# First feed-forward block of an encoder layer: one plain inner chunk instead of three, and one more unit of seven products

## The chip, the cores and the metric

The kernel runs on one core of one Trainium2 chip. A core has TensorE (PE in the profile, with PEld for its weight loads), VectorE (DVE), ScalarE (ACT), GpSimd (POOL) and SyncE (SP), each with its own in-order list of instructions, and 16 DMA engines that all of them share. The metric is the device time of one execution in microseconds (us).

## The reference

One layer of a bidirectional encoder on 512 tokens of width 1024, in float32. A conditioning vector gives nine shift, scale and gate vectors (`mod`); then come a gated feed-forward block, two attention mixers side by side, and a second feed-forward block. Only the first block is touched:

```python
mod = silu(c) @ w_mod + b_mod                # 9 vectors of 1024
h = rmsnorm(x, norm_ffn1) * (1 + sc1) + sh1
gate, up = split(h @ w_ffn1_in)              # 1024 x 5632: 2816 gate, 2816 up
x = x + 0.5 * g1 * ((silu(gate) * up) @ w_ffn1_out)
```

## The kernel before

**Products in three parts.** Activations lie with their features on the 128 partitions and the 512 tokens along the free axis. Every float32 operand of a large product is split into a rounded high part and a low part (`split_from`: ACT copies the high part, DVE subtracts it to get the low one), and a product is three matmuls: high by high, high by low, low by high (L174 to L176, 512 columns wide). A weight tile of 128x1024 comes by a DMA of 512 KB into a tile `raw` or `u`, and its parts go to one of four slots of two tiles `high` and `low` (L185 and L186 of the profile).

**The inner width.** The 2816 inner columns of the first block are 22 chunks of 128. For each chunk there are a gate product and an up product, both over the eight blocks of 128 features. Chunks 0 to 2 are computed in the opening, where DVE still works out the shift and scale vectors (L272, with the columns of `w_mod` as they arrive) and h itself (L346 to L351). After the opening come `PLAIN` pairs less the three chunks already done, computed plainly: in the kernel before, `PLAIN` is 3, so chunks 3, 4 and 5, each of 48 matmuls of 512 columns. `finish` then takes silu of the gate (ACT, L725), multiplies (DVE, L726) and splits the result.

**Units of seven products.** The rest goes in units, each of two chunks of gate and two of up. A unit splits weights and h into 2 by 2 blocks and forms its result by seven products of half the columns instead of eight, with sums of weight blocks and sums of h blocks as operands. Each product is 24 matmuls of 256 columns (L444 to L446). Its products and their h operands are `s1` by n1, `a11` by b11, `a12` by b21, `s2` by n2, `s3` by t3, `s4` by b22, `a22` by t4. The sums n1, n2, t3, t4 are formed once by DVE in `h_sum` (L574 and L576) and split. The sums of weights are made by DMAs that add: SP loads a21 into a tile (L478), POOL issues a DMA that adds a22 (L480), which gives s1; after s1 has been split, POOL issues another that adds a11 into the same tile, which gives s2, and after that one that adds a12, which gives s4; a21 added onto the tile of a11 gives s3 (all L499). After a product ACT copies its PSUM bank aside where it is needed later (L521), or DVE adds it to others (L523, L528, L531). The products a11, s2, s3 and a22 of one unit share one bank, so the matmuls of s2 wait for the copy of a11, and those of s3 for the copy of s2.

**Order.** SP and POOL issue in the order of the program. Instructions of PE, ACT and DVE in this part are ordered by the framework's scheduler when the kernel is built; on the chip each engine keeps that order. `run_items` goes through a written list of products; each has its load asked for (`ASK`) and its parts made (`MAKE`) some products ahead, and before each product `side1` adds 0.27 to a credit; a full credit loads one more column of `w_mod` into one of two places and works an earlier one off on DVE (L272). A third column load waits on SP until DVE has worked off the first.

**After the units.** The output product of the block (`Out1`, L174 to L176) runs over groups of chunks: 0 to 5, 6 to 11, 12 to 15, 16 to 21. In the kernel before, the list is unit 3, group one, units 4 and 5, group two, and so on to unit 10. One product of the next unit's `s1`, `a11` and `a12` stands among those of the current one.

Of the kernel before, what the change touches and what calls it, by code (L numbers as in the profile page):

```python
# [106 lines left out]
MIX_ASIDES = 0, 0, 0, 0, 0, 0, ASIDE, ASIDE  # L107

CHUNKS = (range(0, 6), range(6, 12), range(12, 16), range(16, 22))
PLAIN, LAST_1 = 3, 4  # L110


EARLY, NEXT, SIDE, LATER = 3, 3, 0.27, 4
# [21 lines left out]
def layer(ctx: ExitStack, tc: tile.TileContext, a: dict):  # L135
# [16 lines left out]
    def f2():  # L152
        return sbuf("f2", [P, T], F32, F2)

    def b8(dt=F32R):
        return sbuf("b8", [P, 4, T], dt, 12)

    def u4(dt=F32R):
        return sbuf("u4", [P, 2, T], dt, 6)
# [13 lines left out]
    def mm3(out, wh, wl, xh, xl, first, last):  # L173
        PE.matmul(out, wh, xh, start=first, stop=False)  # L174
        PE.matmul(out, wh, xl, start=False, stop=False)  # L175
        PE.matmul(out, wl, xh, start=False, stop=last)  # L176
# [7 lines left out]
    def split_from(hi, lo, src):  # L184
        S.copy(hi, src)  # L185
        V.tensor_tensor(lo, src, f(hi), ALU.subtract)  # L186
# [18 lines left out]
    def load_split(src, n=1024, spare=False, aside=0):  # L205
        raw = sbuf("raw", [P, 1024], F32, RAW)
        if spare:
            hi, lo = (u4().rearrange("p a b -> p (a b)") for _ in range(2))
        else:
            hi, lo = high_low(aside=aside)  # L210
        nc.sync.dma_start(raw[:, 0:n], src)
        split_from(hi[:, 0:n], lo[:, 0:n], raw[:, 0:n])
        return hi, lo
# [207 lines left out]
    def pair_banks():  # L421
        return (bank("acc"), bank("sc"))
# [111 lines left out]
    def run_items(items):  # L534

        due, at, now = [], [], 0.0  # L540
        for u, q, ks, also in items:
            at.append(now)
            for do, ahead in ((u.ask, u.ASK), (u.prepare, u.MAKE)):
                if q in ahead:
                    due.append((now - ahead[q], len(due), do, q))
            now += u.length
        due.sort(key=lambda d: d[0:2])

        def begin(n):

            for d in [d for d in due if d[0] <= at[n]]:
                _, _, do, p = d
                if do.__name__ == "ask" or p in do.__self__.ready or len(holders) < HILO:
                    due.remove(d)
                    do(p)

        for n, (u, q, ks, also) in enumerate(items):
            begin(n)
            if also is not None:
                also()  # L560
            u.multiply(q, ks)
            if ks is None or u.depth - 1 in ks:
                u.after(q)
            begin(n)
# [6 lines left out]
    def sub(out, p, q, negated):  # L571

        if negated:
            V.scalar_tensor_tensor(out, p, -1.0, q, ALU.mult, ALU.subtract)  # L574
        else:
            V.tensor_tensor(out, p, q, ALU.subtract)  # L576
# [10 lines left out]
    def h_sum(t):  # L587

        p, q = SUMS[t]
        hq[t] = hq[q if t in ("t3", "t4") else p]  # L590

        h_op[t] = [u4() for _ in range(2)] if t == "n1" else b8()
        for i in range(2):
            r = slice(i * T, (i + 1) * T)
            sub(hq[t][:, r], hq[p][:, r], hq[q][:, r], t in NEGATED)
        for i in range(2):
            v = hq[t][:, i * T : (i + 1) * T].rearrange("p (k q) -> p k q", k=2)
            o = h_op[t][i] if t == "n1" else h_op[t][:, 2 * i : 2 * i + 2, :]
            split_from(o[:, :, T1], o[:, :, T2], v)
# [118 lines left out]
    def act_of(p):  # L718
        if p not in act1:
            act1[p] = b8()  # L720
        return act1[p]

    def finish(q, out):
        s, m = f2(), f2()
        S.activation(s, out[0], AF.Silu)  # L725
        V.tensor_tensor(m, s, out[1], ALU.mult)  # L726
        t = act_of(q // 2)
        split_from(t[:, q % 2, :], t[:, 2 + q % 2, :], m)
# [23 lines left out]
    def in_unit1(p):  # L752
        srcs = {q: a["w1u"][p - PLAIN, i] for i, q in enumerate(("a11", "a12", "a21", "a22"))}
        u = Unit(srcs, 4, h1_operand, in_post1, p % 2)
        u.p, u.in_order = p, ('s2', 's4')
        return u
# [49 lines left out]

    items1 = []

    def item1(u, q, ks=None):
        items1.append((u, q, ks, side1))  # L810

    credit, asked = [0.0], []

# [3 lines left out]
    def column(columns):  # L817

        if columns:
            v, c = columns.pop(0)  # L820
            w = room[len(columns) % len(room)] if columns is not later else None
            asked.append((v, c, mod_load(v, c, w)))
        if asked and (len(asked) > COLUMNS[columns is rest] or not columns):
            mod_col(*asked.pop(0), in_order=columns is not later)

    def side1(n=SIDE):

        while small_loads and len(rest) < 20:
            nc.sync.dma_start(*small_loads.pop())
        credit[0] += n  # L830
        while (rest or asked) and credit[0] >= 1.0:
            credit[0] -= 1.0
            column(rest)

    with tc.manual_schedule(engines={mybir.EngineType.SP, mybir.EngineType.Pool}):
        for q in range(3):
            finish(q, out1[2 * q : 2 * q + 2])
        sums1 = ["n1", "n2", "t3", "t4"]
        units1 = {p: in_unit1(p) for p in range(PLAIN, NH)}
        for q in range(3, 2 * PLAIN):  # L840

            w = loaded1 or [load_split(a["w1i"][q - 3, k], aside=ASIDE * (q == 5)) for k in range(2)]
            loaded1 = None
            out = pair_banks()
            for k in range(NC):
                wh, wl = w[k // 4]
                for i in range(2):
                    o = (k % 4) * 256 + i * P
                    mm3(out[i], wh[:, o : o + P], wl[:, o : o + P], hh[k], hl[k], k == 0, k == NC - 1)
            for _ in range(2):  # L850
                if sums1:
                    h_sum(sums1.pop(0))
            finish(q, out)
            if q == 3:
                units1[PLAIN].ask("s1")
            elif q == 4:
                units1[PLAIN].prepare("s1")
            side1(1.0)
        begun = PLAIN
        for n, chunks in enumerate(CHUNKS):  # L860


            final = n + 1 == len(CHUNKS)
            for p in range(begun, max(chunks.stop // 2, PLAIN + 1)):
                u, nxt = units1[p], units1.get(p + 1)
                if p == PLAIN:
                    item1(u, "s1")
                    item1(u, "a11")
                elif p > begun:
                    item1(units1[p - 1], "a22")  # L870
                if p == PLAIN or p > begun:
                    item1(u, "a12")
                item1(u, "s2")
                if nxt:
                    item1(nxt, "s1")
                item1(u, "s3")
                item1(u, "s4")
                if nxt:
                    item1(nxt, "a11")
            item1(u, "a22")  # L880
            if nxt:
                item1(nxt, "a12")
            begun, nxt = p + 1, nxt or u
            out = Out1(chunks, "acc" if nxt.odd != final else "sc", final)
            if final:
                first = range(len(chunks) - 2)
                for m in range(2):
                    item1(out, m, first)
                for m in range(2):
                    item1(out, m, range(len(chunks) - 2, len(chunks)))  # L890
            for m in range(2 if final else 0, NC - LAST_1 if final else NC):
                item1(out, m)
        run_items(items1)
        last1 = []
        for m in range(NC - LAST_1, NC):
            out.prepare(m)
            last1.append((m, lambda po, r, m=m: out.products(m, po, r, range(out.depth))))
        while rest or asked:
            column(rest)
# [931 lines left out]
    u = units[2]  # L1831
# [19 lines left out]
    for v, p in seq:  # L1851
# [7 lines left out]
        u = v  # L1859
# [77 lines left out]
```

## Time and profile before

| | us |
|---|---|
| median of three runs | 1066.88 |
| lowest and highest | 1066.68, 1067.96 |
| span of the profiled execution | 1066.6 |
| PE busy in it | 1047.0 |
| DVE, ACT, POOL busy | 795.7, 566.6, 155.0 |

The page gives no other time for the profiled execution than its span, from the first to the last instruction, 0.28 us below the median. The granted TensorE clock is 1.00 throughout. Times in the text are microseconds from the start of the span.

In the timeline a row gives start, duration, engine, line, operation, output<-input and shapes, and in brackets the idle time of the engine before it with what ended it. Matmuls overlap: one of 512 columns is shown with 0.39 us, but starts follow each other by 0.227 to 0.234 us, and the starts are what counts.

### The profile page before, as it was taken

How to read it: one execution, taken by the hardware profiler on the slowest of the kernel's cores; microseconds unless marked ns; L12 is line 12 of the kernel's file. 1: busy time of each engine (PE TensorE's matmuls, PEld its weight loads, DVE VectorE, ACT ScalarE, POOL GpSimd, SP SyncE). 2: the span in 40 equal slices, each digit the busy share in tenths (PEclk: the TensorE clock that was granted, in tenths of full speed). 3: DMA queues.
4: the chain of work that ended last, by engine and by line, in shares of the span. 5: the costliest groups of instructions: out<-in, count | busy, mean ns of one | idle time of the engine just before them, and what ended most of it. 6: DMA issues, size and time to landing. Idle time of an engine off the chain costs nothing.

```text
span 1066.6 us, 18660 instructions
## 1 busy us (share of the span) xinstructions
PE 1047.0 (98%) x7316; PEld 953.3 (89%) x7316; DVE 795.7 (75%) x1459; ACT 566.6 (53%) x928; POOL 155.0 (15%) x174
## 2 busy tenths in 40 slices
PE   7999999999999999999999999999999999999998
PEld 5689889899899998888777878989999999999997
DVE  6985666666796679858864578976889777877867
ACT  5564334344354342667676755534766646654553
POOL 1100010100110100443211100001011211112210
PEclk9999999999999999999999999999999999999999
DMA  9968687866975459696356852974498998999974
GB/s 332 362 205 208 207 211 189 264 155 195 281 181 160 164 200 409 215 270 160 99 120 166 239 160 85 351 242 118 101 232 200 215 230 217 220 219 213 219 146 124
DMA packets 69084, 220.92 MB, mean 207 GB/s; under 512 B 8194, under 2 KB 10882, under 8 KB 68995
## 3 DMA queue, kind: packets, MB, share of 16 engines
q1 hardware_dynamic: 46512, 146.52, 38.2%
q0 software_dynamic: 19488, 68.70, 34.9%
q10 hardware_dynamic: 2994, 4.51, 1.2%
q8 instruction: 57, 0.93, 0.3%
q14 instruction: 33, 0.26, 0.1%
HBM read 209.46 MB, written 10.23 MB: 206 GB/s over the span
## 4 chain that ended last, share of the span: by engine, by line
PE 79%; DVE 8%; issue 5%; DMA 3%; ACT 3%; POOL 1%; SPq 0%; ACTq 0%; DVEq 0%; POOLq 0%
PE acc L444 5%; PE acc L446 5%; PE acc L445 5%; PE sc L174 5%; PE sc L175 5%; PE sc L176 5%; PE sc L446 5%; PE sc L444 5%; PE sc L445 5%; PE acc L174 4%; PE acc L176 4%; PE acc L175 4%; PE sc L182 2%; PE acc L1048 2%; PE acc L1049 2%
## 5 line engine op out<-in xcount | busy, mean ns | idle before, releaser
L185 ACT CAST high<-raw 128x1024 fp32r<-128x1024 f32 (+2 forms) x162 | 158.3, 986 | 165.9 <-PE acc L445 38.8
L186 DVE TENSOR_TENSOR low<-raw,high 128x1024 fp32r<-128x1024 f32 (+2 forms) x162 | 183.7, 1141 | 61.2 <-ACT high L185 60.2
L444 PE MATMUL acc<-b,high 128*128 128x256 f32 x508 | 141.0, 278 | 0.3 <-DVE f L523 0.3
L446 PE MATMUL acc<-b,low 128*128 128x256 f32 x508 | 140.6, 277 | 0.2 <-DVE low L186 0.2
L445 PE MATMUL acc<-b,high 128*128 128x256 f32 x508 | 140.6, 277 | 0.1
L444 PE MATMUL sc<-b,high 128*128 128x256 f32 x500 | 138.5, 277 | 1.8 <-ACT f L521 1.8
L446 PE MATMUL sc<-b,low 128*128 128x256 f32 x500 | 138.6, 277 | 1.1 <-DVE low L186 1.1
L445 PE MATMUL sc<-b,high 128*128 128x256 f32 x500 | 138.4, 277 | 0.0
L186 DVE TENSOR_TENSOR low<-u,high 128x1024 fp32r<-128x1024 f32 (+1 forms) x73 | 87.5, 1200 | 28.4 <-ACT high L185 27.1
L185 ACT CAST high<-u 128x1024 fp32r<-128x1024 f32 (+1 forms) x73 | 75.5, 1035 | 56.5 <-PE sc L175 15.9
L174 PE MATMUL sc<-b,high 128*128 128x512 f32 (+1 forms) x280 | 100.8, 360 | 0.0
L175 PE MATMUL sc<-b,high 128*128 128x512 f32 (+1 forms) x280 | 100.4, 359 | 0.0
L176 PE MATMUL sc<-b,low 128*128 128x512 f32 (+1 forms) x280 | 100.2, 358 | 0.0
L444 PEld LDWEIGHTS acc<-b,high 128*128 128x128 f32 x508 | 95.4, 188 | 0.8 <-DVE f L523 0.5
L444 PEld LDWEIGHTS sc<-b,high 128*128 128x128 f32 x500 | 94.0, 188 | 2.2 <-ACT f L521 2.2
L445 PEld LDWEIGHTS acc<-b,high 128*128 128x128 f32 x508 | 95.5, 188 | 0.4 <-DVE b L1725 0.3
L446 PEld LDWEIGHTS acc<-b,low 128*128 128x128 f32 x508 | 95.4, 188 | 0.4 <-DVE low L186 0.4
L446 PEld LDWEIGHTS sc<-b,low 128*128 128x128 f32 x500 | 93.9, 188 | 1.5 <-DVE low L186 1.5
L445 PEld LDWEIGHTS sc<-b,high 128*128 128x128 f32 x500 | 93.9, 188 | 0.0
L174 PE MATMUL acc<-b,high 128*128 128x512 f32 (+1 forms) x248 | 92.7, 374 | 0.0
L176 PE MATMUL acc<-b,low 128*128 128x512 f32 (+1 forms) x248 | 90.0, 363 | 0.0
L175 PE MATMUL acc<-b,high 128*128 128x512 f32 (+1 forms) x248 | 89.8, 362 | 0.0
(369 smaller groups left out, 2676.4 us busy)
## 6 DMA issues: line engine op xcount, KB each, us to landing
u<-w_mod SPq DMA_DIRECT2D x40, 512.0 KB, 7.6
b<-w_mod SPq DMA_DIRECT2D x32, 512.0 KB, 6.0
raw<-w2i SPq DMA_DIRECT2D x31, 512.0 KB, 5.9
u<-w2i POOLq DMA_DIRECT2D x31, 512.0 KB, 6.6
u<-w1u POOLq DMA_DIRECT2D x24, 512.0 KB, 7.1
raw<-w1u SPq DMA_DIRECT2D x24, 512.0 KB, 6.8
raw<-w1o SPq DMA_DIRECT2D x24, 384.0 KB, 4.5
raw<-w_gate SPq DMA_DIRECT2D x16, 512.0 KB, 6.8
```

The lines of the kernel that those rows point to most:

```text
L174: PE.matmul(out, wh, xh, start=first, stop=False)
L175: PE.matmul(out, wh, xl, start=False, stop=False)
L176: PE.matmul(out, wl, xh, start=False, stop=last)
L182: PE.matmul(out, of[j][a], of[j][b], start=i == 0, stop=i == 2)
L185: S.copy(hi, src)
L186: V.tensor_tensor(lo, src, f(hi), ALU.subtract)
L444: PE.matmul(out, wh[:, s], xh, start=first and j == 0, stop=False, skip_group_check=True)
L445: PE.matmul(out, wh[:, s], xl, start=False, stop=False, skip_group_check=True)
L446: PE.matmul(out, wl[:, s], xh, start=False, stop=last and j == 1, skip_group_check=True)
L1048: PE.matmul(out[t][:, 0:n], hh[k][:, ht], wh[:, o : o + n], start=k == 0, stop=False)
L1049: PE.matmul(out[t][:, 0:n], hh[k][:, ht], wl[:, o : o + n], start=False, stop=False)
```

## The change

`PLAIN` goes from 3 to 2. Chunk 3 alone is computed plainly; chunks 4 and 5 become unit 2. The units are now 2 to 10, nine instead of eight, and the list is unit 2, group one, units 3, 4 and 5, group two, and then as before. The loads of `w1i` for chunks 4 and 5 go (four of 512 KB); the loads and adding DMAs of a unit come (eight transfers of 512 KB).

With one chunk left, what stood between the three has to go elsewhere. The weights of the first unit's s1 are asked for before chunk 3 and made after it; n1 and n2 are formed at chunk 3, t3 before the product s1, t4 before a11. Of the three column loads, one now stands before chunk 3 and two after it.

```diff
-PLAIN, LAST_1 = 3, 4
+PLAIN, LAST_1 = 2, 4
...
-    def item1(u, q, ks=None):
-        items1.append((u, q, ks, side1))
+    def item1(u, q, ks=None, sums=None):
+        def do():
+            side1()
+            if sums:
+                h_sum(sums)
+
+        items1.append((u, q, ks, do))
...
             finish(q, out1[2 * q : 2 * q + 2])
+        side1(1.0)
         sums1 = ["n1", "n2", "t3", "t4"]
         units1 = {p: in_unit1(p) for p in range(PLAIN, NH)}
+        units1[PLAIN].ask("s1")
         for q in range(3, 2 * PLAIN):
...
             finish(q, out)
-            if q == 3:
-                units1[PLAIN].ask("s1")
-            elif q == 4:
-                units1[PLAIN].prepare("s1")
-            side1(1.0)
+            units1[PLAIN].prepare("s1")
+            side1(2.0)
...
                 if p == PLAIN:
-                    item1(u, "s1")
-                    item1(u, "a11")
+                    item1(u, "s1", sums="t3")
+                    item1(u, "a11", sums="t4")
```

## The prediction

> **What bounds the kernel now.** I read the totals of the page first, then the chain that ended last, then the waits of PE.
>
> ```profile
> span 1066.6 us, 18660 instructions
> PE 1047.0 (98%) x7316; PEld 953.3 (89%) x7316; DVE 795.7 (75%) x1459; ACT 566.6 (53%) x928; POOL 155.0 (15%) x174
> ...
> PE 79%; DVE 8%; issue 5%; DMA 3%; ACT 3%; POOL 1%; SPq 0%; ACTq 0%; DVEq 0%; POOLq 0%
> ...
> PE sc L444 <- ACT f L521: 1.8, 1, 1.8
> PE sc L446 <- DVE low L186: 1.1, 2, 0.8
> ...
> core 0: 1066.6 us, clock 1.000
> ```
>
> PE is busy in all but 19.6 us, and its longest waits among the units are 1.8 and 0.8 us. So PE is the bound: matmuls taken away are time gained, and a wait that PE does not have now is time lost, for nothing later has slack to give it back. The question is whether the last thing before each product still arrives in time once 22 us of cover in front of the units are gone.
>
> **PE's own work.** The timeline of PE gives the starts of chunks 3, 4 and 5 and those of the ten products that follow.
>
> ```profile
> 57.01 0.39 PE L174 MATMUL acc<-b,high 128*128 128x512 f32 x1
> 67.89 0.39 PE L174 MATMUL acc<-b,high 128*128 128x512 f32 x1
> 78.76 0.40 PE L174 MATMUL acc<-b,high 128*128 128x512 f32 x1
> 89.96 0.28 PE L444 MATMUL sc<-u,high 128*128 128x256 f32 x1
> 92.79 0.28 PE L444 MATMUL sc<-b,high 128*128 128x256 f32 x1
> 100.97 0.28 PE L444 MATMUL acc<-u,high 128*128 128x256 f32 x1
> 103.77 0.28 PE L444 MATMUL sc<-b,high 128*128 128x256 f32 x1
> 109.23 0.28 PE L444 MATMUL acc<-b,high 128*128 128x256 f32 x1
> 111.95 0.28 PE L444 MATMUL sc<-b,high 128*128 128x256 f32 x1
> 114.67 0.28 PE L444 MATMUL op<-b,high 128*128 128x256 f32 x1
> 117.39 0.40 PE L174 MATMUL sc<-b,high 128*128 128x512 f32 x1
> ```
>
> Removed: chunks 4 and 5, 96 matmuls, 89.96 - 67.89 = 22.07 us. Added: the seven products of one unit, 168 matmuls. Unit 3 fills 89.96 to 100.97, 103.77 to 109.23 and 111.95 to 114.67 (between them lie s1, a11 and a12 of the next unit): 11.01 + 5.46 + 2.72 = 19.19 us. With every operand in time the change is worth 22.07 - 19.19 = 2.88 us.
>
> **The opening.** There DVE sets the pace, and it splits n1 in the middle of it:
>
> ```profile
> 43.25 0.69 DVE L186 TENSOR_TENSOR u<-b,u 128x512 fp32r<-128x512 f32 x1
> 48.53 0.69 DVE L186 TENSOR_TENSOR u<-b,u 128x512 fp32r<-128x512 f32 x1
> 49.26 0.75 DVE L351 SCALAR_TENSOR_TENSOR b<-f,mod,b 128x512 fp32r<-128x512 f32 x1
> 50.06 0.51 PE L689 MATMUL acc<-b,high 128*128 128x512 f32 x1
> ```
>
> L351 at 49.26 releases PE at 50.06, and from there PE runs through to 57.01. As built, the changed kernel forms n1's parts after the opening; the first of the two places is empty and the second holds a subtraction (L576) of the same shape. One place of 43.86 - 43.25 = 0.61 us goes from DVE's chain. Bounds: 0, if the columns of `w_mod` come no sooner, and 0.61; I take 0.61, since DVE does not stand idle there. Chunk 3 then runs from 56.40 to 67.28.
>
> **Wait A: the low part of the first s1.** These are DVE's rows of before:
>
> ```profile
> 56.70 1.88 DVE L726 TENSOR_TENSOR f<-f,sc 128x512 f32<-128x512 f32 x3
> 65.13 1.21 DVE L186 TENSOR_TENSOR low<-u,high 128x1024 fp32r<-128x1024 f32 x1
> 66.27 2.35 DVE L186 TENSOR_TENSOR low<-raw,high 128x1024 fp32r<-128x1024 f32 x2
> 69.74 1.27 DVE L272 CUSTOM_DVE_ANT_0 b<-b,ka,begin 128x1024 f32<-128x1024 f32 x1
> 70.94 0.08 DVE L272 DVE_READ_ACCUMULATOR2_ANT mod<- 128x1 f32 x1
> 79.03 0.69 DVE L726 TENSOR_TENSOR f<-f,sc 128x512 f32<-128x512 f32 x1 [0.65 <-PE sc L176]
> ```
>
> At 65.13 DVE makes the low part of s1, 25 us before PE uses it. In the changed kernel as built, DVE's order after the opening is:
>
> ```
> L726 x3, L186 (parts of chunks 0 to 2) x3, L186 (n1) x2, L574 x2, L272, L186 (n2) x2, L272, L186 (t3) x2, L574
> L726 f2_92<-f2_91,sc_87        (chunk 3)
> L186 low_99<-u4_85,high_92     (s1)
> ```
>
> So s1's low part stands behind the `finish` of chunk 3. A half-tile operation takes 0.60 us of DVE's queue (three in 1.8), a column 1.2 (69.74 to 70.94), a low part 1.15. The row at 56.70 moves to 56.09; fifteen half tiles and two columns end at 56.09 + 9.0 + 2.4 = 67.5. L726 of chunk 3 can start 0.27 us after its chunk ends (79.03; chunk 5 starts at 78.76), at 67.55, so the low part lies between 68.15 and 69.35. PE can issue two matmuls of s1 after 67.28 and then waits from 67.5 to 69.4: 1.9 us. Even with an idle DVE the 0.27, 0.60 and 1.15 us would leave 1.75, so A lies between 1.75 and 2.5 (a slower column load).
>
> **Wait B: the copy of a11's bank.** This is the largest term. s2 starts from an addition onto the tile of s1 that POOL issues only when s1's low part is done. POOL's next transfer adds a22 to the next unit's tile. In the changed kernel ACT's order is
>
> ```
> L521 f2_99<-acc_98             (copy of s1)
> L185 high_92<-u4_85            (s2, waits for its addition)
> L185 b8_100<-b8_65             (t4)
> L185 high_92<-u4_94            (next s1, waits for its addition)
> L521 f2_102<-acc_101           (copy of a11)
> ```
>
> and s2's matmuls write acc_101, so the copy of a11 and with it PE stand behind two transfers. In the kernel before those additions had the two plain chunks to land in:
>
> ```profile
> 66.88 0.86 POOL L499 DMA_DIRECT2D u<-w1u  x1 [16.41 <-ACT high L185]
> 78.28 0.86 POOL L480 DMA_DIRECT2D u<-w1u  x1 [10.54 <-DMA u<-w1u]
> DMA to landing us min/median/max: 5.2/7.5/9.2
> DMA to landing us min/median/max: 6.9/6.9/6.9
> DMA to landing us min/median/max: 4.5/6.1/7.6
> 95.66 1.05 ACT L185 CAST high<-raw 128x1024 fp32r<-128x1024 f32 x1 [1.26 <-issue]
> 96.62 0.58 ACT L521 COPY f<-sc 128x512 f32<-128x512 f32 x1
> ```
>
> (The three landing lines are those of L499, L480 and L478 between 60 and 100 us.) POOL comes 0.4 to 0.5 us after the low part, at 69.8; its issue takes 0.86, so the next unit's addition is issued at 70.7. It is the second in line, and loads of SP are under way beside it:
>
> ```profile
> 71.05 0.33 SPq L243 DMA_DIRECT2D b<-w_mod  x1
> 71.48 0.39 SPq L478 DMA_DIRECT2D raw<-w1u  x1
> 71.92 0.42 SPq L478 DMA_DIRECT2D u<-w1u  x1
> 72.44 1.81 SPq L478 DMA_DIRECT2D raw<-w1u  x3
> ```
>
> This burst waited for the first worked-off column (70.94). In the changed kernel the first column ends at 63.4, so the burst starts at 63.5 and its six loads, landing up to 7.6 us after issue (the third landing line), are still under way at 71. Nearest rows: 5.2 us (alone) to 9.2 (behind others); I take 9.2, as this addition is behind another one and beside loads. It lands at 79.9, its cast ends at 80.95, the copy at 81.5. PE has s1 done at 69.4 + 22 x 0.118 = 72.0, a11 and a12 (2.73 each) at 77.45. B = 81.5 - 77.45 = 4.0 us; with 5.2 us it would be 0.2.
>
> The Trainium skill speaks of this price: "DMA: Bandwidth & Descriptors", section "Anatomy of one DMA — SWDGE (gpsimd) path", fits a DMA of GpSimd as 2.0 us plus its bytes over 436 GB/s, which is an estimate of 3.2 us for 512 KB. By that B would be nothing. The rows here never show less than 5.2 us for these adding transfers, so the measurement decides.
>
> **Wait C: what comes late after that.** s2 then ends at 84.2 and the next s1 at 87.0. On DVE the low part of s3 (its addition is third on POOL, landing near 82.6) ends at 84.9, L528 at 85.5. On ACT the silu (L740) waits for L528, then comes a cast, then the copy of s2, done near 87.65, for which s3 waits: 0.7 us. DVE goes on with two columns and two low parts before that of s4, done near 91.35, where PE stands at 90.65: 0.7 us. C = 1.4, with bounds 0 (the order has slack if the additions land early) and 2.5.
>
> **What costs nothing.** t3 and t4 are needed at 84 us and later and are formed by 73. The act parts of chunks 4 and 5, which now come from unit 2, are first read in group one after 12 matmuls (2.7 us) of the first output product, and the product a12 of the next unit (2.72) lies before that: 5.4 us for two DVE and one ACT operations of 0.6. If that cover fell, each output product would lose up to 2 us once. Four transfers of 512 KB more on the DMA engines lie beside PE, except where B and C count them. The extra 7 credits of 0.27 move two columns to earlier units; the two waits of 1.8 and 0.8 us stand at the end of their groups and I leave them as they are, plus or minus 1 us.
>
> **Sum.** -0.61 (opening) - 2.88 (PE) + 1.9 (A) + 4.0 (B) + 1.4 (C) = +3.8. Span 1066.6 + 3.8 = 1070.4; the median lies 0.28 above the span: 1070.7.
>
> **Rivals.** (1) The additions land early, in 5.2 us each: B is 0.2, A and C stay, +0.0, 1066.9. It decides where the second one lands before 75.9. For it speaks the 66.88 row's idle surroundings, against it SP's burst. (2) The other side, faster: the additions are early and the order of ACT and DVE keeps up (C = 0), so that only A is left: -0.61 - 2.88 + 1.9 = -1.6, 1065.3, and 1064.7 where the two waits at the ends of groups also shrink. The point where it decides is the copy of a11 by 77.45. DVE's static order, with two columns ahead of s4, speaks against it. (3) The clock drops: B leaves PE idle for about 4 us, over twice the 1.8 of the row above, and if the product that follows then runs at half rate, 24 matmuls take 2.7 us more: 1073.4. No row here shows a granted clock under 1.00. By the Trainium skill ("TensorE: Matmul & The Clock Gate", section "Part 1: The HAM clock gate (the "warmup" mystery)") a free-running window of about 3.4 us without work brings half the clock; a 4 us gap would hold such a whole window in a minority of phases only. That the change does not do what it says is excluded: as built, PE has 96 matmuls of 512 columns fewer and 168 of 256 more.
>
> **How the numbers follow.** Forecast (1068.6 to 1072.6 by its bounds) 0.56; rival 1 0.20; rival 2 0.10; rival 3 0.14. The predicted time is the forecast's 1070.7. Within 0.2%, about what a measurement of this kernel can tell from no change, is 1064.7 to 1069.0: rival 1, half of rival 2, and a small lower part of the forecast, 0.27. Faster is the other half of rival 2 and a little, 0.06. Slower is the rest, 0.67. The range drops rival 2 and the far end of rival 3: 1066.7 to 1074.0.
>
> **What would show it.** Right: chunk 3 starts near 56.4 us; the first L446 of s1 waits about 1.9 us for DVE L186; PE waits about 4 us before s2 for ACT L521, with the cast of a `u` tile that a DMA of L480 released just ahead on ACT; smaller waits before s3 and s4; all else as before. Wrong: no wait for L521 there (rival 1 or 2), a granted clock under 1.00 near 80 us (rival 3), or new waits of PE after 100 us, which I have at nothing.

## The result and the profile after

The changed kernel takes 1080.67 us (median of 4 runs, 1079.89 to 1082.49) against 1066.78 us beside it: a ratio of 1.0133, 95% interval 1.0121 to 1.0145. It is slower by 13.9 us where 3.8 were forecast, and lies above the range that ends at 1074.0.

First the page of the changed kernel, with the same lines as before the change: span, busy times, the chain that ended last.

```profile
span 1080.6 us, 18823 instructions
...
PE 1051.8 (97%) x7388; PEld 959.0 (89%) x7388; DVE 800.3 (74%) x1465; ACT 571.6 (53%) x934; POOL 158.9 (15%) x178
...
PE 74%; DVE 10%; DMA 6%; issue 6%; ACT 3%; POOL 1%; SPq 0%; DVEq 0%; POOLq 0%; ACTq 0%
```

The profiled execution is the longest of the four (1082.49 us). PE idles 28.8 us instead of 19.6, and is busy 4.8 us more although it has less to compute. Both have to be explained. The waits of PE in the changed kernel (what waited, for what; total, times, longest) name four that the kernel before does not have:

```profile
PE acc L444 <- ACT f L521: 6.1, 1, 6.1
...
PE acc L446 <- DVE low L186: 1.8, 1, 1.8
PE acc L176 <- DMA low<-w_gate: 1.6, 1, 1.6
...
PE acc L174 <- ACT high L988: 1.4, 1, 1.4
```

The first is wait B, the second wait A. The other two lie in the attention stage, far behind the change. The starts on PE in the changed kernel (chunk 3, the first s1, s2, group one):

```profile
55.63 0.39 PE L174 MATMUL acc<-b,high 128*128 128x512 f32 x1
...
66.51 0.28 PE L444 MATMUL acc<-u,high 128*128 128x256 f32 x1
...
83.10 0.58 PE L444 MATMUL acc<-b,high 128*128 128x256 f32 x1 [6.13 <-ACT f L521]
...
104.66 0.40 PE L174 MATMUL acc<-b,high 128*128 128x512 f32 x1
```

The matmul at 83.10 takes 0.58 us instead of 0.28: the clock is at half. Next the busy time by stretches (width, then PE, PEld, DVE, ACT, POOL busy, then the granted clock, DMA share and GB/s). The first stretch reaches from chunk 3 to the first statistic of the second norm (L337), that is, over all units and groups. Changed kernel:

```profile
55.63:365.91 310.28, 300.95 (x2101) 280.24 (x2100) 217.58 (x311) 138.31 (x186) 33.06 (x40) 0.99 0.76 212
...
525.00:555.00 30.00, 27.02 (x121) 19.40 (x120) 18.59 (x53) 18.26 (x39) 9.01 (x9) 0.89 0.58 140
...
80.00:90.00 10.00, 6.90 (x39) 6.90 (x40) 7.01 (x9) 5.78 (x8) 1.73 (x2) 0.66 0.98 206
```

Kernel before, the same stretches of work:

```profile
57.01:360.38 303.37, 300.84 (x2029) 276.28 (x2028) 210.79 (x302) 131.99 (x178) 29.62 (x36) 1.00 0.74 206
...
520.00:550.00 30.00, 29.20 (x165) 22.64 (x164) 22.88 (x66) 21.24 (x53) 9.61 (x9) 1.00 0.57 141
```

So the 14.0 us between the two profiled spans come in two places. In the first block: chunk 3 starts 1.38 us earlier, the stretch from there is 310.28 - 303.37 = 6.91 us longer, together +5.5. In the attention stage, around 525 to 555 us, 121 matmuls are done in 30 us where 165 were, at a mean clock of 0.89. The rest of the program, with all that it loses, makes 14.0 - 5.5 = +8.5.

How wait B came about is seen in the rows of POOL and ACT of the changed kernel:

```profile
69.13 0.86 POOL L499 DMA_DIRECT2D u<-w1u  x1 [17.89 <-ACT high L185]
69.67 1.21 POOL L480 DMA_DIRECT2D u<-w1u  x1
70.63 1.14 POOL L499 DMA_DIRECT2D raw<-w1u  x1
...
78.02 1.05 ACT L185 CAST high<-u 128x1024 fp32r<-128x1024 f32 x1 [5.74 <-DMA u<-w1u]
...
81.52 1.04 ACT L185 CAST high<-u 128x1024 fp32r<-128x1024 f32 x1 [1.93 <-DMA u<-w1u]
82.47 0.58 ACT L521 COPY f<-acc 128x512 f32<-128x512 f32 x1
```

And the landing times of the first two of these transfers, from the view of the tile `u`:

```profile
DMA to landing us min/median/max: 8.9/10.3/11.8
```

The structure is the forecast's: three additions one behind another on POOL, the next unit's second in line, its cast ahead of the copy of a11 on ACT. The second one was issued 1.0 us earlier than forecast and landed 11.8 us after its issue, not 9.2.

### The profile page after: what moved, and what is told of

Same layout as the page of the kernel before. It is cut to its first block, busy times and chain, and to the rows that moved or that the text cites. A ratio compares the mean times of both kernels' runs of the same rounds, so it can differ in the third digit from the quotient of the medians.

```text
span 1080.6 us, 18823 instructions
## 1 busy us (share of the span) xinstructions
PE 1051.8 (97%) x7388; PEld 959.0 (89%) x7388; DVE 800.3 (74%) x1465; ACT 571.6 (53%) x934; POOL 158.9 (15%) x178
## 4 chain that ended last, share of the span: by engine, by line
PE 74%; DVE 10%; DMA 6%; issue 6%; ACT 3%; POOL 1%; SPq 0%; DVEq 0%; POOLq 0%; ACTq 0%
PE acc L444 6%; PE acc L445 6%; PE acc L446 6%; PE acc L174 5%; PE acc L176 5%; PE acc L175 5%; PE sc L446 4%; PE sc L444 4%; PE sc L445 4%; PE sc L175 3%; PE sc L176 3%; PE sc L174 3%; PE acc L1052 2%; PE sc L182 2%; PE acc L1054 2%
## 5 line engine op out<-in xcount | busy, mean ns | idle before, releaser
L444 PE MATMUL acc<-b,high 128*128 128x256 f32 x548 | 153.3, 280 | 6.4 <-ACT f L521 6.1
L445 PE MATMUL acc<-b,high 128*128 128x256 f32 x548 | 152.7, 279 | 0.1
L446 PE MATMUL acc<-b,low 128*128 128x256 f32 x548 | 152.6, 279 | 0.1
L186 DVE TENSOR_TENSOR low<-u,high 128x1024 fp32r<-128x1024 f32 (+1 forms) x76 | 91.1, 1200 | 30.3 <-ACT high L185 29.2
L444 PEld LDWEIGHTS acc<-b,high 128*128 128x128 f32 x548 | 104.0, 190 | 7.1 <-ACT f L521 6.5
L185 ACT CAST high<-u 128x1024 fp32r<-128x1024 f32 (+1 forms) x76 | 78.6, 1036 | 56.2 <-PE sc L445 12.2
L174 PE MATMUL acc<-b,high 128*128 128x512 f32 (+1 forms) x280 | 105.7, 378 | 1.4 <-ACT high L988 1.4
L176 PE MATMUL acc<-b,low 128*128 128x512 f32 (+1 forms) x280 | 103.1, 369 | 1.6 <-DMA low<-w_gate 1.6
L445 PEld LDWEIGHTS acc<-b,high 128*128 128x128 f32 x548 | 104.2, 190 | 0.4 <-DVE b L1729 0.3
L446 PEld LDWEIGHTS acc<-b,low 128*128 128x128 f32 x548 | 103.9, 190 | 0.3 <-DVE low L186 0.3
L175 PE MATMUL acc<-b,high 128*128 128x512 f32 (+1 forms) x280 | 102.9, 368 | 0.0
L175 PE MATMUL sc<-b,high 128*128 128x512 f32 (+1 forms) x216 | 75.6, 350 | 0.3 <-DVE b L186 0.3
L174 PE MATMUL sc<-b,high 128*128 128x512 f32 (+1 forms) x216 | 75.8, 352 | 0.0
L176 PE MATMUL sc<-b,low 128*128 128x512 f32 (+1 forms) x216 | 75.3, 349 | 0.0
```

What stands on the lines that cost most here:

```text
L444: PE.matmul(out, wh[:, s], xh, start=first and j == 0, stop=False, skip_group_check=True)
L445: PE.matmul(out, wh[:, s], xl, start=False, stop=False, skip_group_check=True)
L446: PE.matmul(out, wl[:, s], xh, start=False, stop=last and j == 1, skip_group_check=True)
```

## The experiments

All runs below have kernels before beside them on the same chip (medians 1066.8 to 1067.3). The start of chunk 3 scatters between 54.2 and 57.5 us over the profiled executions (59.7 in the one where a wait stands before it), largely since the opening's first matmul (L689) starts anywhere from 18.3 to 20.8; so stretches are counted from chunk 3 on. This table is the summary, its stretches each from one profiled execution; "half clock" is the time from chunk 3 to L337 that the trace records at a granted clock of 0.5.

| kernel | median, us | chunk 3 to L337 | PE idle in it | half clock |
|---|---|---|---|---|
| before | 1066.8 | 303.4 | 2.5 | 0 |
| changed | 1080.7 | 310.3 | 9.3 | 6.8 |
| changed, slots as before | 1074.3 | 309.1 | 7.7 | 6.8 |
| before, slots as changed | 1077.0 | 301.2 | 0.4 | 0 |
| changed, four gate offsets | 1076.1 | 310.2 | 8.6 | 6.8 |
| slots, copy before cast | 1073.7 | 308.7 | 7.4 | 2 x 3.4 |
| slots, filler | 1078.2 | 312.7 | 7.1 | 3.4 |
| slots, filler (second form) | 1074.2 | 307.3 | 3.2 | 0 |
| slots, both additions early | 1069.0 | 303.1 | 4.0 | 0 |
| order by hand | 1069.1 | 305.3 | 5.1 | 6.8 |
| by hand, s4 last | 1068.6 | 304.4 | 3.7 | 3.4 |
| by hand, s2's cast early | 1066.1 | 302.2 | 3.3 | 0 |
| and next s1's low part early | 1066.8 | 302.1 | 3.7 | 0 |

**The late loss: a rotation that was shifted.** The parts of every weight go to five slots in rotation (five, not the four of the description ahead of the change), each 1024 columns; a weight may be put some columns (its offset, 16 for some) into its slot, and then reaches 16 columns into the next one, unless it is in the last slot, which has 16 spare columns. Two chunks took four turns of the rotation, a unit takes seven, and slots still held are skipped; counted in the program, from the attention stage on everything lies two slots further. In the kernel before the last gate weight with offset 16 is in the last slot and the next, without offset, in the first. In the changed kernel they are in slots 1 and 2: the next weight's slot begins inside the previous weight, and can't be written until PE has used that.

```diff
-    turn, holders = [0], {}
+    turn, holders = [3], {}
```

> The changed kernel with one number changed: the rotation of the five weight slots starts at slot 3 instead of slot 0, so that from the attention stage on every weight lies in the slot that it had in the kernel before. Theory S (slots): the unit that replaces two chunks takes two more turns of the rotation, a gate weight then lies 16 columns into the slot of the next one, and the waits and half-clock windows between 525 and 550 us come from that: the 7.3 us lost there come back, 1080.7 - 7.3 = about 1073.4 us, no half-clock window after 500 us, the first block's loss (5.5 us at its end) unchanged. Rival L (the later loss follows from the later start, or from the clock alone): nothing comes back, about 1080.7 us.

From the second norm on PE's 5092 matmuls come in the order of the kernel before. Measured: 1074.27 us (1073.98 to 1074.81), 6.4 less. The stretch of the attention stage:

```profile
525.00:555.00 30.00, 29.21 (x163) 22.54 (x162) 22.83 (x65) 22.45 (x54) 9.64 (x9) 1.00 0.55 141
```

163 matmuls again, and the full clock. From the second norm to the end the profiled executions take 706.3 us in the kernel before, 714.7 in the changed kernel and 706.4 here. The first block keeps its waits (5.6 us for B, 1.8 for A) and its half clock. The opposite, the shift alone in the kernel before:

```diff
-    turn, holders = [0], {}
+    turn, holders = [2], {}
```

> The kernel before with the rotation started at slot 2, so that from the attention stage on every weight lies in the slot that it has in the changed kernel; the first block computes three plain chunks as before. Theory S: the later loss appears alone, 1066.8 + 7.3 = about 1074.1 us, with half-clock windows between 515 and 550 us and none in the first block. Rival L: about 1066.8 us, nothing at half clock.

Measured: 1077.01 us (1074.48 to 1080.44), a ratio of 1.0098 (1.0072 to 1.0123). The loss came without the change. The waits of PE in the profiled execution, its fastest, and then the stretch:

```profile
PE acc L174 <- ACT f L725: 2.3, 1, 2.3
...
PE acc L174 <- ACT high L984: 1.3, 1, 1.3
...
PE acc L176 <- DMA low<-w_gate: 1.3, 1, 1.3
```

```profile
520.00:550.00 30.00, 27.41 (x136) 20.17 (x134) 19.04 (x55) 20.35 (x43) 9.44 (x9) 0.94 0.66 157
```

The two gate waits are those of the changed kernel. The first line is a side effect of the shift at chunk 3, made up by shorter waits behind it (PE idles 0.4 us from there to L337 instead of 2.5). In this execution (1074.48) 5.9 us are lost between the second and the third norm (376.5 us from L337 to L337 instead of 370.6); the loss of 10.2 us by the medians is larger, and where the longer executions lost the rest was not profiled.

Is it the overlap or only another order? The third edit leaves the slots alone and lets the step from offset 16 to none fall on the last slot:

```diff
-            wh, wl = load_main(a["w_gate"][j], ASIDE * (j == EARLY_A))
+            wh, wl = load_main(a["w_gate"][j], ASIDE * (EARLY_A <= j < EARLY_A + 4))
```

> The changed kernel with its own slots; only the gate weights with offset 16 are four instead of one, so that the step from offset 16 to offset 0 falls between the last slot, which has 16 spare columns, and the first, and no gate weight overlaps the next one's slot. Theory S with the overlap as its mechanism: the two waits between 534 and 545 us and their half-clock windows go, about 1073.4 us. Rival: it is the order of instructions that the slots lead to, not this overlap: about 1080.7 us.

Measured: 1076.05 us (1075.24 to 1076.74), 4.6 less than the changed kernel, with the attention stage as before:

```profile
525.00:555.00 30.00, 29.26 (x165) 22.56 (x164) 22.83 (x65) 21.20 (x53) 9.64 (x9) 1.00 0.56 141
```

So that overlap is the larger part: 4.6 of the 6.4 us by the medians, and 6.7 of 8.1 us by the profiled executions between the second and the third norm (370.6 us in the kernel before, 378.9 in the changed one, 370.8 with the slots as before, 372.2 here). The rest is not shown at one place; part of it is two waits for DVE, 1.0 us together, near 700 us, which the first run does not have. Just before them lie the weights of the last branch (`w_ya`), where the program steps from offset 16 to none once more, on the same two slots and with the same exchange on ACT; this edit leaves that as it is.

How the overlap works is seen in ACT's casts of gate weights. In the kernel before, the weight with offset 16 (first row) is followed by the next gate's 8.4 us later:

```profile
480.56 1.03 ACT L984 CAST high<-raw 128x1024 fp32r<-128x1024 f32 x1
489.00 1.07 ACT L984 CAST high<-raw 128x1024 fp32r<-128x1024 f32 x1
```

In the changed kernel no cast comes there:

```profile
486.93 1.03 ACT L988 CAST high<-raw 128x1024 fp32r<-128x1024 f32 x1
503.40 1.06 ACT L988 CAST high<-raw 128x1024 fp32r<-128x1024 f32 x1
```

The order as built has the next gate's cast behind those of the three gates after it, 46 us after the first row, at 533.02. The addition that completes its low part leaves POOL at 536.87, and PE has it at 544.52; it waits for both parts. With the four offsets the next cast follows after 8.2 us again (485.77 to 493.94); in the kernel before with the shifted slots after 16.8 (481.31 to 498.07), much as in the changed kernel (16.5). The changed kernel's rows of that place:

```profile
533.02 1.07 ACT L988 CAST high<-raw 128x1024 fp32r<-128x1024 f32 x1
...
534.15 0.50 PE L174 MATMUL acc<-b,high 128*128 128x512 f32 x1 [1.35 <-ACT high L988]
...
536.87 0.94 POOL L990 DMA_DIRECT2D low<-w_gate  x1 [2.58 <-ACT low L989]
...
544.52 0.50 PE L176 MATMUL acc<-b,low 128*128 128x512 f32 x1 [1.63 <-DMA low<-w_gate]
```

Behind each the clock is at half for 3.41 us (535.2 to 538.6 and 545.5 to 548.9 in its records), which costs half of that each. Waits (3.0 less the 0.8 that the stretch had) and clock (3.4) make 5.6 of the 7.0 us by which the changed kernel falls behind the first run there (one matmul past the place starts at 569.69 and at 562.95, and 0.25 of lead at 530 is lost too); the rest is not read from a row.

All later experiments have the slots of the first one, so 1074.3 us is their base.

**Wait B: the copy, or the weight behind it?** In the next run only two instructions of ACT change places (and some of DVE after them): the copy of a11 comes before the cast of the next s1.

```diff
+        units1[PLAIN + 1].MAKE = {**Unit.MAKE, "s1": 2}
+        units1[PLAIN + 1].in_order = ("s1", "s2", "s4")
         begun = PLAIN
```

> The kernel of the first run (1074.3 us) with one exchange in ACT's order: the copy of the second product's bank stands before the cast of the next unit's s1 instead of behind it; PE's order is the same. The forecast's reading of wait B (the copy is late only because of that cast): the wait falls from 5.6 us to what the fourth product's own weight leaves. Its cast began 1.1 us after PE was free and its low part was ready 3.4 us after, so about 3.3 us, and the next unit's s1 then waits some 0.8 us: 1.5 us less, about 1072.8 us, and 2.5 us less again (1070.3 us) if the shorter wait leaves the clock at full speed. Rival Q (the weight of the fourth product is what is late, with POOL's queue behind it): little changes, 1073.5 to 1074.3 us.

Measured: 1073.66 us (1071.57 to 1074.61). Waits of PE between 56 and 125 us, and then the stretches behind:

```profile
PE acc L444 <- ACT f L521: 5.3, 2, 2.9
```

```profile
80.00:90.00 10.00, 7.32 (x48) 7.12 (x48) 6.33 (x8) 5.43 (x8) 1.72 (x2) 0.83 1.00 203
90.00:100.00 10.00, 9.55 (x69) 9.55 (x70) 7.50 (x11) 3.48 (x6) 0.86 (x1) 0.83 0.94 241
```

One wait of 5.6 became two of 2.9 and 2.4, the second one for the copy before s3, and the half clock split likewise. The forecast's cause (the copy behind that cast) is half of B only. In the other half the copy stands behind the cast of s2's own weight, which ACT begins at 78.69 us, when its addition has landed 8.6 us after its issue; and what is freed is waited for two products on. The next run takes the additions out of POOL's queue: both s1 are asked for before chunk 3.

```diff
         units1[PLAIN].ask("s1")
+        units1[PLAIN + 1].ask("s1")
```

> The kernel of the first run with the next unit's s1 asked for beside the first unit's, before chunk 3, so that both additions leave POOL's queue before the addition for the fourth product's weight. Theory Q (POOL's queue and the transfers of the burst make wait B): the fourth product's addition has the queue to itself and lands some 3 us earlier, the cast of the next s1 has long been done, wait B 0 to 1.5 us and the clock at full speed: 1074.3 - 4.8 - 2.5 = about 1067.0 us (1066.0 to 1069.5). Rival (the landing is set by the transfer itself, 8.9 us from its issue at 69.1 us): wait B about 3 us, 1069.5 to 1072 us.

Measured: 1068.97 us (1067.43 to 1071.32), a ratio of 1.0018 (1.0005 to 1.0030) to the kernel before: 5.3 us less for one line. The waits of PE there, 56 to 125 us:

```profile
PE acc L444 <- ACT f L521: 1.2, 1, 1.2
PE acc L444 <- ACT high L185: 1.0, 1, 1.0
PE sc L444 <- ACT high L185: 1.0, 1, 1.0
PE acc L446 <- DVE low L186: 0.5, 1, 0.5
```

The addition for s2 was alone and landed 5.3 us after its issue, against 8.9 in the changed kernel and 8.0 in the base, and the next s1 is cast at 68.94 us, ahead of the whole unit's copies. B is gone: s2 starts at 78.39 us, right behind a12. The line of 1.2 us is the wait of s3 for the copy of s2 (at 85.07), the line of 0.5 the low part of s4: that is the forecast's wait C, at both its places. In A's place PE waits twice for 1.0 us, for the high parts of the two s1. The clock stays at 1.00. So B came from the next unit's addition that stood in front of the first unit, by its place in POOL's queue and by its cast ahead of the copy on ACT.

**What the half clock costs.** PE gets 24 matmuls of 512 columns that nobody reads, between a12 and the wait.

```diff
-                item1(u, "s2")
+                item1(u, "s2", sums="fill" if p == PLAIN else None)
...
+            if sums == "fill":
+                spare = bank("tp")
+                with tc.issue_after(ended[0]):
+                    for i in range(24):
+                        PE.matmul(spare, hh[0][:, 0:P], hh[0], start=True, stop=True)
```

> The kernel of the first run with 24 matmuls of 512 columns whose result nobody reads (24 x 0.23 = 5.5 us) queued on PE between the third product and the wait of 6.1 us before the fourth (wait B), so that PE works while it waits. Theory C (the half clock from 81.2 to 88.1 us is the answer to PE's idleness in the wait): the clock stays at full speed, the 5.0 us that products ran at half speed cost 2.5 us less, about 1070.9 us, PE's wait before the fourth product shorter by the filler. Rival: the clock drops anyway, or costs nothing: about 1073.4 us as in the first run, or 1 to 2 us above it where the filler ends after the data.

Measured: 1078.20 us (1077.20 to 1083.32). The clock did stay at 1.00 from 80 to 90 us, but as built two small copies on DVE had moved ahead of a weight's low part, and they wait for the last loads of SP. PE's waits in this run, then DVE's rows:

```profile
PE acc L448 <- DVE low L186: 5.9, 2, 4.1
```

```profile
94.60 0.17 DVE L918 CAST posf<-pos 128x4 f32<-128x4 int32 x1 [2.97 <-DMA pos<-pos]
...
95.15 1.23 DVE L186 TENSOR_TENSOR low<-raw,high 128x1024 fp32r<-128x1024 f32 x1
```

Two copies of 0.17 us kept DVE from that low part for 3.5 us (91.63 to 95.15), and PE waited 4.1 us. With them pinned behind the first output update:

> The filler of 24 matmuls once more, with the two small copies of positions and sinks pinned on DVE behind the first output update, so that the filler no longer pulls them ahead of a weight's low part; the rest of the order is that of the first run (1074.3 us). Theory C: no half clock after 80 us, 2.5 us less, about 1071.8 us. Rival (the half clock costs nothing, or comes with the wait whatever PE does): about 1074.3 us.

Measured: 1074.18 us (1071.66 to 1075.96), no different from the base. In the profiled execution (1071.66) no half clock is left and the first block is 1.8 us shorter than in the base:

```profile
55.30:362.58 307.28, 304.04 (x2126) 282.20 (x2125) 217.71 (x311) 138.52 (x186) 33.05 (x40) 1.00 0.77 214
...
80.00:90.00 10.00, 9.02 (x67) 8.13 (x66) 6.84 (x8) 6.76 (x9) 1.72 (x2) 1.00 1.02 209
```

That PE's idleness brings the half clock is shown. Its price, 2.5 us by the rows of the changed kernel (5.0 us computed at half), is not: the one profiled execution gained 1.8 us, while over whole executions the mean granted clock rose (0.998 to 1.000 in the four here, 0.995 to 0.998 in the base) and the median did not move. That stays open.

**What the change is worth when nothing waits.** The order was written out by hand, with the two small copies pinned as above: both s1 and the raw weights of a11 and a12 asked for before chunk 3; DVE and ACT in program order between the opening and the first unit, with the low part of s1 before n1 and n2; the casts of s2, s3 and the next s1 behind the copies.

```diff
+        with tc.manual_schedule(engines={mybir.EngineType.DVE, mybir.EngineType.Activation}):
+            units1[PLAIN].ask("s1")
+            units1[PLAIN + 1].ask("s1")
+            for q in ("a11", "a12"):
+                units1[PLAIN].ask(q)
...
+                units1[PLAIN].prepare("s1")
                 for _ in range(2):
                     if sums1:
                         h_sum(sums1.pop(0))
+                side1(2.0)
                 finish(q, out)
+        units1[PLAIN].MAKE, units1[PLAIN + 1].MAKE = {**Unit.MAKE, "s2": 2}, {**Unit.MAKE, "s1": 2}
+        units1[PLAIN].in_order = ("s2", "s3", "s4")
+        units1[PLAIN + 1].in_order = ("s1", "s2", "s4")
```

> The changed kernel put in order by hand: slots as before; both s1 and the first unit's two raw weights asked for before chunk 3; between the opening and the first unit DVE and ACT in the order of the text, with the low part of s1 before the sums n1 and n2; the casts of the fourth and fifth product's weights and of the next s1 behind the copies; the two small copies pinned as above. Theory: what the change is worth without waits A and B and without half clock is PE's own work, 2.9 us less than the kernel before, about 1064 us (1063 to 1066). Rival: DVE is full from 50 to 72 us, and the sums that now come later make a wait of the same size at the second or fourth product: 1067 us or more.

Measured: 1069.11 us (1066.95 to 1071.65). A and B are gone; in their place PE waits 4.4 us for the weight of s4. Waits of PE, then rows of POOL and ACT:

```profile
PE acc L444 <- ACT high L185: 4.4, 1, 4.4
```

```profile
61.22 0.86 POOL L499 DMA_DIRECT2D u<-w1u  x1 [7.41 <-DVE low L186]
...
73.80 0.86 POOL L499 DMA_DIRECT2D u<-w1u  x1 [10.84 <-DVE low L186]
...
70.04 0.59 ACT L521 COPY f<-acc 128x512 f32<-128x512 f32 x1 [1.24 <-PE acc L446]
70.53 1.06 ACT L185 CAST high<-u 128x1024 fp32r<-128x1024 f32 x1
```

s1, s2 and s4 are made by additions into one tile: the addition for s2, issued at 61.22, had landed at 66.6, but its cast stood behind the copy of s1; so the addition for s4 left only at 73.80 and landed at 82.9. Two ways out were tried. First, the product s4 moved behind a22:

```diff
-                item1(u, "s4")
+                if p > PLAIN:
+                    item1(u, "s4")
...
             item1(u, "a22")
+            if n == 0:
+                item1(u, "s4")
```

> The kernel put in order by hand (the run before, 1069.1 us, which still waited 4.4 us for the weight of s4 and lost 2.2 us to the half clock behind it), with one exchange: the first unit's s4 comes after its a22 instead of before the next unit's a11, so that the third addition into the same tile has two products (5.4 us) more. Theory: s4's weight was 4.4 us late only because the three additions into one tile follow each other (about 9 us from issue to landing, then cast and low part, each) and the unit starts one chunk after the opening; with the product moved the wait and the half clock go: 1069.1 - 4.4 - 2.2 = about 1062.5 us (1061.5 to 1065), 3 to 5 us less than the kernel before. Rival: the late copy of s4's sum delays the output product behind it, or another weight is next in line with 2 to 4 us: 1066 us or more.

Measured: 1068.57 us (1066.28 to 1072.24), 1.0009 (1.0000 to 1.0018). s4 waits no more, but group one does, for the activation that comes out of s4, as the rival said:

```profile
PE acc L174 <- ACT b L185: 1.8, 1, 1.8
PE acc L175 <- DVE b L186: 0.8, 1, 0.8
```

Second, the cast of s2 free to go as soon as its addition has landed and asked for four products ahead again instead of two, with the products in their old order:

```diff
-        units1[PLAIN].MAKE, units1[PLAIN + 1].MAKE = {**Unit.MAKE, "s2": 2}, {**Unit.MAKE, "s1": 2}
-        units1[PLAIN].in_order = ("s2", "s3", "s4")
+        units1[PLAIN + 1].MAKE = {**Unit.MAKE, "s1": 2}
+        units1[PLAIN].in_order = ("s3", "s4")
```

> The kernel put in order by hand again (1069.1 us; wait of 4.4 us for the weight of s4), now with the products in their own order and the cast of s2's weight free to go when its addition has landed (66.6 us in that run) instead of behind the copy of s1 (70.5 us): the addition for s4 can start some 4 us earlier. Theory (three additions into one tile, each landing 5 to 9 us after its issue, are the chain that sets the first unit): s4's weight is ready by about 80 us, the wait falls to 0 to 1 us and the half clock goes, 1069.1 - 4.0 - 2.2 = about 1063 us (1062 to 1065). Rival: DVE and ACT stall for the landing, n2 and the raw weights behind the column loads come later, and 2 us or more is waited elsewhere: 1066 us or more.

Measured: 1066.12 us (1063.77 to 1070.06) against 1066.85, 0.9996 (0.9983 to 1.0008): no difference. One longer wait is left between 56 and 125 us, and from chunk 3 to L337 PE is busy 2.0 us less than in the kernel before:

```profile
PE sc L446 <- DVE low L186: 2.0, 1, 2.0
```

```profile
54.21:356.37 302.16, 298.87 (x2101) 277.82 (x2100) 219.05 (x316) 137.52 (x186) 32.19 (x39) 1.00 0.78 215
```

The last run lets that low part go earlier too (the next s1 without its place in ACT's order):

```diff
-        units1[PLAIN + 1].MAKE = {**Unit.MAKE, "s1": 2}
-        units1[PLAIN + 1].in_order = ("s1", "s2", "s4")
+        units1[PLAIN + 1].MAKE = {**Unit.MAKE, "s1": 3}
```

> The run before (1066.1 us; its one wait over 0.7 us in the first block was 2.04 us for the low part of the next unit's s1, whose addition had landed long before and which stood behind two sums on DVE), with that cast and low part let go as soon as the planner likes: on DVE the low part now stands before the two sums (1.29 us). Theory: DVE's order alone makes that wait, which falls by 1.3 us: about 1064.8 us, 1 to 2 us below the kernel before, so that the change is worth something near PE's own 2.4 us once nothing waits. Rival: the two sums are then late for the sixth product, the wait only moves: 1066 us.

Measured: 1066.76 us (1064.79 to 1068.97), 0.9999 (0.9988 to 1.0009). That wait fell to 0.8, and 1.2 and 1.0 us appeared at two other products. No version beat the kernel before: the 2 us and more of PE's work that the change saves were in no version seen in the time, since waits of 1 us or more were left in each.

## Why the prediction was wrong

The sign and the mechanism in the first block were right; a term was too small, and a whole place was missing.

- **PE's own work**, forecast -2.88: right in kind, 0.5 to 1.1 us too large. In the runs without half clock and filler PE is busy 299.10, 298.87 and 298.43 us from chunk 3 to L337 against 300.84: -1.7 to -2.4.
- **The opening**, -0.61: right in size. From the first to the last start of its matmuls (L689) it takes 36.49 us against 36.98, 0.49 less; the six other versions with the change that are not ordered by hand take 36.48 to 36.51, and the kernel before with shifted slots 36.98. The other 0.9 of the 1.38 us by which chunk 3 started early are a first matmul that happened to start early: luck.
- **Wait A**, 1.9: right, 1.75 in the trace, at the named instruction.
- **Wait B**, 4.0: right in place and cause, but 6.1. The mis-sized term is "I take 9.2": the nearest row was an addition behind others, but here three leave POOL within 2 us and land 8.9 to 13.4 us after issue, the one in question 11.8. That is 2.6 more, less 1.0 for the earlier issue; the rest is PE, which was ready 0.5 us earlier. The Trainium skill's fit ("DMA: Bandwidth & Descriptors", section "Anatomy of one DMA — SWDGE (gpsimd) path") gives an estimate of 3.2 us for each; the runs show 5.2 at the least.
- **Wait C**, 1.4: nothing in the changed kernel, because B's delay hides it. It is there when B shrinks (2.4 us before s3 in the run with the copy before the cast) and, with B gone, at the two places named and near their size (1.2 us before s3 and 0.5 at s4, with both additions early). So it should not have been added to B.
- **The clock** was rival 3, with a chance of 0.14, and it came: half clock from 81.2 to 88.1 us, two steps of 3.41. B was longer than the 4 us of its condition, and the estimate of 2.7 us stands beside 2.5 by the rows.
- **The waits at the ends of groups**, "plus or minus 1 us": 1.1 less (0.88 and 0.56 instead of 1.78 and 0.76).
- Together: -1.38 - 2.4 (PE) + 1.75 + 6.13 - 1.1 + 2.5 = 5.5, the measured delay of the second norm. Rival 3 (6.5 us above the kernel before) comes within 1.0 us of it by luck: its B is 2.1 too small, and against that stand its C of 1.4, the 1.1 at the ends of groups and the early start.
- **The step that failed** is the last one: "all else as before", and new waits after 100 us "which I have at nothing". The change was followed up to the first group and no further. But it changes a counter that all later weights use: two slots further on, one gate weight overlaps the slot of the next, that one's high part is made 46 us behind the previous one's instead of 8, and PE waits for it in the attention stage, some 450 us after the waits of the first unit. Of the 8.5 us lost behind the first block in the profiled execution nearly all come back with the rotation restored, 6.4 by the medians, 4.6 of them by the overlap alone; shifting the rotation in the kernel before costs at least as much. Nothing in the profile of before shows this; the rotation and the offsets in the program do, together with the order as built.
- **Without that step** the forecast would still have been too low: with the rotation restored the kernel takes 1074.3 us, 3.6 above the forecast, by B and the clock less C.
- **Two smaller numbers.** "The median lies 0.28 above the span" does not hold: where the time and the span of one execution are both listed, the time is 1.7 us or more above the span. It drops out of the difference. And the bounds given for the opening, A and C add up to 1069.1 to 1073.0 us, not to 1068.6 to 1072.6.

## What to carry to other kernels

When a change alters how many buffers of a shared rotation are used, count the turns and compare which buffer each later user gets: a stage that the change does not touch can lose more than the stage that it does. A chain of dependent transfers (here load, add, split, add, split, add) needs its lead time as cover in front of the first consumer, and when one wait in it is taken away the next one in the chain shows; price the chain, not each wait by itself. A short idle of PE can be followed by half clock: behind the two gate waits, 3.0 us together, matmuls ran at half for 6.8 us, which by the rows costs another 3.4. So ask of each new wait what the clock does next.

## What the runs showed of the hardware

- The granted clock falls in steps of 3.41 us. Waits of 5.6 to 6.1 us (three profiled runs) and 4.4 us brought two steps, waits of 2.9, 2.4 and 4.1 one each; waits of 1.75 (A, in six profiled runs), 2.0 and 2.3 none. But 1.8 and 0.8 close together (the run with s4 last) brought one, and in the attention stage of the changed kernel 1.35 and 1.63 us were enough for one each, while in the kernel before with shifted slots only one of two waits of 1.3 brought one. So the length of a wait alone does not decide. The Trainium skill ("TensorE: Matmul & The Clock Gate", section "Part 1: The HAM clock gate (the "warmup" mystery)") has the half clock come after an idle window of about 3.4 us: the length of the steps agrees, the idle time needed does not, since neither gate wait fills half of such a window.
- Half clock comes and goes between executions too: seven of the thirteen profiled ones have a step or two between 12.4 and 19.2 us, in the opening, and the executions of the kernel before have mean granted clocks from 0.994 to 1.000.
- An adding DMA of 512 KB issued by POOL landed 5.2 to 5.5 us after its issue at the quickest (alone on POOL, in five profiled runs), after 8.8 and 9.1 us in two runs that issued another 2.9 us behind it, and after 12.8 to 13.5 us as third of three issued within 2 us (six profiled runs).
- PE work put into a wait kept the clock at 1.00 there (two profiled runs), where the same wait without it brought the half clock.
